# A hybrid decoder step on one core: seven pairs of its first projection with half the contraction in seven products of sums, variances inverted on 72 partitions, and two places in the gate reordered

## The chip, the cores and the metric

The kernel runs on one core of one Trainium2 chip. A core has engines with instruction streams of their own, each worked off strictly in order: TensorE (PE; its weight loads are counted as PEld), VectorE (DVE), ScalarE (ACT), GpSimd (POOL) and SyncE (SP), which here only issues DMAs. POOL issues DMAs too, on a queue of its own. The metric is the device time of one execution in microseconds (us), as the median of the runs.

## The reference, cut to what matters

576 tokens (512 of a prompt, and 8 sequences of 8 samples) go through one layer with 2048 channels. Channels are kept on the partitions, tokens on the free axis.

```python
h = rmsnorm(x, g_mix)
z = h @ w_in                                   # 2048 x 4096: a_val, a_gate, u, v
a = a_val * sigmoid(a_gate)                    # group A: 8 heads of 128 channels
a_out = silu(head_layernorm(causal_dwconv(concat(hist, a), w_dw_a, b_dw_a)))   # 31 taps
u = gelu(u); v_n = head_layernorm(gelu(v))     # group B: 8 heads of 128 channels
b_out = u * (tril(w_s[h]) @ v_n + b_s[h])      # over chunks of 128 positions
x = x + concat(a_out, b_out) @ w_out
up = rmsnorm(x, g_ffn) @ w_up                  # then a convolution of 3 taps, SiLU gate
x = x + (silu(conv(up)[:5632]) * conv(up)[5632:]) @ w_down
gate = sigmoid(rmsnorm(x, g_ple) @ w_ple_gate)
x = x + gate * (p @ w_ple_proj)
y = rmsnorm(x, g_final)                        # also the convolution states and v_n are outputs
```

`head_layernorm` subtracts the mean over a head's 128 channels and multiplies by 1/sqrt(variance + eps).

## The kernel before, in words

Every fp32 product is made from three matmuls: weights and activations are split into a high part and a rest (`wh`, `wl`, `xh`, `xl`), and `wh·xh + wh·xl + wl·xh` is summed in PSUM. One weight tile is 128x128, a token half is 288 columns, so a tile costs 6 matmuls of 288 columns, 3 for each half. The weights come in one stream of 512 KB units (8 tiles) on SP's queue into 5 buffers `raw`. A **piece** is 4 tiles: ACT makes `wh` of it (`prepare`, L279), then DVE makes `wl` (L283). There are 4 buffers of each, so the `wh` of piece s waits until PE has used piece s-4.

The stages in order, with the times of the trace: the first group (`gate(0)`, `val(0)`, `gate(1)` together, to 45 us); the rest of the first projection (to about 451 us), where for i = 2 to 7 the columns `vee(i-2)`, `you(i-2)` (v and u of group B), `gate(i)`, `val(i)` (group A) follow each other and `vee(6)`, `you(6)` come after them; a last group with `vee(7)` and `you(7)` together; `w_out` in two parts (`out` without the late channels `LATE`, then `out2`); the up-projection (680 to 1655 us), down-projection (to 2165 us), the gate in pairs of columns (to about 2316 us) and the two last gate columns with the final norm. The up-projection and the gate pairs already use the scheme that the change brings to the first projection: products of sums of weight tiles with sums of activations, seven for eight (`seven`, L879 to L881).

A main loop emits the matmuls in this order. After every 4 tiles it calls `deal()`, which hands out side work against a credit: first one step from `chain`, then steps from `urgent` or `todo`, each with a cost. `settle()` takes steps until a condition holds. A scheduler at compile time then fixes the order of each engine's instructions: it goes by the order of emission and by when its own model of times thinks an operand is ready. On the chip each engine holds to that order. `tc.issue_after(x)` keeps an instruction behind x.

The side work of group A's head i: `gated` (sigmoid), `val_done` (multiply, and `settle` until head i-3 has ended), then 31 `tap`s. Each tap is two DVE instructions, one on the prompt (L499, 128x512) and one on the samples (L501, 128x64). Then the steps of `chain`: `parts_of`, `centre` (PE and ACT), `square`, `spread` (PE sums the squares with a matrix of ones, ACT takes the root on all 128 partitions, L534), `norm(0)`, `norm(1)` (DVE: RECIPROCAL 128x288, L538, and a multiply, L539) and `fin` (ACT Silu, L543). Group B's head j: `vee_done` (multiply with the RMS factor `r`, L556, Gelu L558 and L559, then `norm`: PE `vps`, ACT L571, DVE `vn`), `you_done`, `mixing` (PE `mps`, DVE).

In the gate, `rms_roots` puts 576 roots on one partition, sends them through DRAM to 72 partitions of 8 (L1007, L1009), and `rms_spread` inverts them there (L1014) and sends them through DRAM to all 128 partitions (L1016, L1018) as `rg`; `gate_done` multiplies by it (L1033). In the tail, `split_12` makes activations of the last columns (ACT L1271, DVE L1272), and L1294 multiplies.

## Time and profile before

| | us |
|---|---|
| median of 3 runs (lowest, highest) | 2378.31 (2376.51, 2378.56) |
| the profiled execution | 2374.55 |
| its span on the core | 2372.9 |
| PE busy | 2353.6 (99%), 17676 matmuls |
| DVE busy | 2065.7 (87%), 3696 instructions |
| ACT busy | 1262.5 (53%), 2342 instructions |
| POOL busy | 265.4 (11%), 414 instructions |

The profile is one execution; its time is the span and what lies around it. A busy PE means that a matmul was under way. Matmuls overlap, so a matmul's own duration is longer than its share of the time. A row of instructions gives the start, the duration, the engine, the line and the tiles, and in brackets how long the engine was idle before it and what ended that.

### The profile page before, as it was taken

To read this page: it belongs to the slowest core of one execution; us is meant where nothing else is said; L and a number is where in the kernel's file an instruction comes from. 1 tells how busy PE (TensorE), PEld (TensorE's weight loads), DVE (VectorE), ACT (ScalarE), POOL (GpSimd) and SP (SyncE) were. 2 spreads that over 40 slices of the span, in tenths; PEclk is the share of its full clock that TensorE was granted. 3 is DMA by queue.
4 is the path that set the end of the run, shared out by engine and by line. 5 is a ranking of instruction groups with operands and counts; after the bars stand their busy time and mean duration, and the time that the engine had idled before them with its cause. 6 is when DMAs were issued, how large, how long until landed. Compare 5 with 4: busy or idle time off the path is not lost.

```text
span 2372.9 us, 45975 instructions
## 1 busy us (share of the span) xinstructions
PE 2353.6 (99%) x17676; PEld 2342.5 (99%) x17676; DVE 2065.7 (87%) x3696; ACT 1262.5 (53%) x2342; POOL 265.4 (11%) x414
## 2 busy tenths in 40 slices
PE   9999999999999999999999999999999999999997
PEld 9999999999999999999999999999999999999997
DVE  7877788887789999999999999999878998778997
ACT  6444544523575555555555555556545455456556
POOL 1000000000120000000000000000222332322112
PEclk9999999999999999999999999999999999999999
DMA  7322222333473333333333333335877776765546
GB/s 246 98 87 82 81 87 80 112 121 101 165 252 108 115 109 117 115 105 110 116 107 110 115 106 110 116 104 169 233 163 172 164 193 160 167 192 171 171 163 221
DMA packets 126392, 326.91 MB, mean 138 GB/s; under 512 B 29580, under 2 KB 46092, under 8 KB 126172
## 3 DMA queue, kind: packets, MB, share of 16 engines
q1 hardware_dynamic: 83068, 230.66, 29.5%
q0 software_dynamic: 37776, 82.68, 14.2%
q10 hardware_dynamic: 5328, 10.63, 1.4%
q8 instruction: 139, 2.28, 0.4%
q14 instruction: 81, 0.66, 0.1%
HBM read 260.45 MB, written 63.46 MB: 137 GB/s over the span
## 4 chain that ended last, share of the span: by engine, by line
PE 93%; issue 2%; DMA 2%; DVE 1%; ACT 1%; POOL 1%; DVEq 0%; POOLq 0%; ACTq 0%
PE acc_up L880 14%; PE acc_up L879 14%; PE acc_up L881 14%; PE acc L1209 10%; PE acc L1211 10%; PE acc L1213 10%; PE acc L839 5%; PE acc L840 5%; PE acc L838 5%; PE acc_gate L879 2%; PE acc_gate L881 2%; PE acc_gate L880 2%; DMA xs<-x1d 0%; POOL x1d L1248 0%; ACT wh L279 0%
## 5 line engine op out<-in xcount | busy, mean ns | idle before, releaser
L279 ACT ACTIVATE wh<-raw 128x512 fp32r<-128x512 f32 x792 | 499.2, 632 | 667.1 <-PE acc L1211 335.7
L879 PE MATMUL acc_up<-sx,wh 128*128 128x288 f32 x2464 | 726.9, 295 | 0.3 <-DVE uu L810 0.3
L881 PE MATMUL acc_up<-sx,wl 128*128 128x288 f32 x2464 | 727.0, 295 | 0.1
L880 PE MATMUL acc_up<-sx,wh 128*128 128x288 f32 x2464 | 726.8, 295 | 0.0
L283 DVE TENSOR_TENSOR wl<-raw,wh 128x512 fp32r<-128x512 f32 x792 | 541.1, 685 | 125.9 <-ACT wh L279 121.7
L879 PEld LDWEIGHTS acc_up<-sx,wh 128*128 128x128 f32 x2464 | 463.9, 188 | 0.6 <-issue 0.5
L880 PEld LDWEIGHTS acc_up<-sx,wh 128*128 128x128 f32 x2464 | 463.9, 188 | 0.1
L881 PEld LDWEIGHTS acc_up<-sx,wl 128*128 128x128 f32 x2464 | 463.1, 188 | 0.6 <-DVE wl L283 0.6
L1209 PE MATMUL acc<-xh,wh 128*128 128x288 f32 x1536 | 330.4, 296 | 0.7 <-ACT wh L279 0.6
L1211 PE MATMUL acc<-xl,wh 128*128 128x288 f32 x1536 | 327.5, 294 | 0.0
L1213 PE MATMUL acc<-xh,wl 128*128 128x288 f32 x1536 | 327.3, 294 | 0.0
L279 ACT ACTIVATE wh<-sy 128x512 fp32r<-128x512 f32 x268 | 170.1, 635 | 232.7 <-PE acc_up L880 155.6
L839 PE MATMUL acc<-sxh,wh 128*128 128x288 f32 x896 | 264.5, 295 | 0.0
L840 PE MATMUL acc<-sxh,wl 128*128 128x288 f32 x896 | 264.2, 295 | 0.0
L838 PE MATMUL acc<-sxh,wh 128*128 128x288 f32 x896 | 264.0, 295 | 0.0
L1209 PEld LDWEIGHTS acc<-xh,wh 128*128 128x128 f32 x1536 | 245.6, 188 | 2.8 <-issue 0.9
L1211 PEld LDWEIGHTS acc<-xl,wh 128*128 128x128 f32 x1536 | 246.5, 188 | 0.3 <-issue 0.2
L1213 PEld LDWEIGHTS acc<-xh,wl 128*128 128x128 f32 x1536 | 245.7, 188 | 0.4 <-issue 0.3
L283 DVE TENSOR_TENSOR wl<-sy,wh 128x512 fp32r<-128x512 f32 x268 | 183.8, 686 | 44.9 <-ACT wh L279 44.3
L499 DVE SCALAR_TENSOR_TENSOR cv<-ep,vec,cv 128x512 f32<-128x512 f32 x240 | 178.6, 744 | 0.0
L840 PEld LDWEIGHTS acc<-sxh,wl 128*128 128x128 f32 x896 | 168.6, 188 | 0.0
L838 PEld LDWEIGHTS acc<-sxh,wh 128*128 128x128 f32 x896 | 168.5, 188 | 0.0
(725 smaller groups left out, 3788.4 us busy)
## 6 DMA issues: line engine op xcount, KB each, us to landing
raw<-in_wstream SPq DMA_DIRECT2D x395, 512.0 KB
x1d<-o POOLq DMA_DIRECT2D x128, 144.0 KB, 4.7
hidd<-hp POOLq DMA_DIRECT2D x44, 288.0 KB, 3.8
xs<-x1d POOLq DMA_DIRECT2D x32, 288.0 KB, 3.9
hq<-hidd ACTq DMA_DIRECT2D x32, 288.0 KB
x<-in_xT SPq DMA_DIRECT2D x16, 288.0 KB
xr<-in_xT SPq DMA_DIRECT2D x16, 288.0 KB
x1d<-x POOLq DMA_DIRECT2D x16, 288.0 KB, 3.5
```

The costliest lines, as they stand in the source:

```text
L279: latest["h"] = nc.scalar.activation(h, src, AF.Copy).ins
L283: latest["l"] = nc.vector.tensor_tensor(out=l, in0=src, in1=h.bitcast(F32), op=ALU.subtract).ins
L499: tc.keep_in_program_order(nc.vector.scalar_tensor_tensor(out=cp, in0=halves(ep[:, k : k + SEQ]), scalar=w, in1=cp, op0=ALU.mult, op1=ALU. ...
L838: nc.tensor.matmul(dst, wh, bh, start=k == 0 and not on, stop=False, skip_group_check=on)
L839: nc.tensor.matmul(dst, wh, bl, start=False, stop=False, skip_group_check=on)
L840: nc.tensor.matmul(dst, wl, bh, start=False, stop=end, skip_group_check=on)
L879: nc.tensor.matmul(place[prod], wh, bh, start=k == 0 and not on, stop=False, skip_group_check=on)
L880: nc.tensor.matmul(place[prod], wh, bl, start=False, stop=False, skip_group_check=on)
L881: nc.tensor.matmul(place[prod], wl, bh, start=False, stop=k == KT // 2 - 1, skip_group_check=on)
L1209: nc.tensor.matmul(accs[n][:, h, :HT], wh, bh[:, h, :], start=st, stop=False)
L1211: nc.tensor.matmul(accs[n][:, h, :HT], wh, bl[:, h, :], start=False, stop=False)
L1213: nc.tensor.matmul(accs[n][:, h, :HT], wl, bh[:, h, :], start=False, stop=sp)
```

## The change

Four things are changed.

1. **Pairs.** For j = 0 to 6 `vee(j)` and `you(j)` form one group `both`. Over k = 0 to 7 (`SUMMED`) the 32 weight tiles (two columns, two token halves) go through seven products, each of a sum of weight tiles with a sum of activation halves (4 x 3 matmuls each: 84 in place of 96). The other 8 k are multiplied plainly (96), in pieces `A0`, `A1`, `B0`, `B1` of 24 matmuls that stand between the products (`MIXED`). A pair has 180 matmuls in place of 192, and 11 pieces in place of 8. DVE adds the weights in place in `raw` (`add_in_place`, 4 of 128x512 a pair), ACT and DVE keep partial results (`kept`) and combine them (`done_a`, `done_b`). The sums of activations (`mix_sums`) are made once, after the first group.
2. **Variances.** `spread` takes the root on one partition only; the 576 roots go through DRAM to 72 partitions of 8, are inverted there, go through DRAM to 128 partitions, and one DVE multiply of 128x576 uses them: four DMAs for each head on POOL's queue. The chains of heads 5 to 7 begin only in the last group.
3. **Room and other places for side work.** The samples' taps are multiplied on ACT (248 instructions of 128x64) and summed on DVE by 32 TENSOR_REDUCE of 9 or fewer taps; results of the heads that aren't late go to DRAM and come back for `w_out` (12 reloads); rows and mixing weights are loaded for each head on POOL's queue rather than at the start on SP's.
4. **Gate and tail.** `rms_spread` is called at the fifth product of the first pair (2 in `PRODS`), not the fourth (7), `rg` is used behind the latest `wl`, and a pause follows. In the tail `split_12` comes after the first half column, behind the latest pieces.

The instructions that move, as each engine executes them (line, operation, output<-inputs with the tile's number, shape):

DVE where head 4 of group A is normalised, before (`wl` are pieces of weights, `cv` and `lnc` the head's root and centred values, `ep` and `es` the next head's convolution):

```order
L477 TENSOR_TENSOR es_4546<-acc_0_4381,ag_4377 128x8x8
L283 TENSOR_TENSOR wl_4555<-raw_4277,wh_4554 128x512
L499 SCALAR_TENSOR_TENSOR cv_4412<-ep_3311,vec,cv_4412 128x2x256
L538 RECIPROCAL cv_3756<-cv_3756 128x288 x2
L539 TENSOR_TENSOR lnc_4481<-lnc_4481,cv_3756 128x288 x2
L501 SCALAR_TENSOR_TENSOR cv_4412<-es_3312,vec,cv_4412 128x2x32
L499 SCALAR_TENSOR_TENSOR cv_4412<-ep_3311,vec,cv_4412 128x2x256
L501 SCALAR_TENSOR_TENSOR cv_4412<-es_3312,vec,cv_4412 128x2x32
```

The same head on DVE now (`vr` holds the 576 values on 72 partitions, `gu` and `kept` belong to the pairs, `raw` are the weights that are added in place):

```order
L322 TENSOR_TENSOR wl_4818<-raw_4553,wh_4817 128x512
L609 RECIPROCAL vr_4493<-vr_4493 72x8
L779 TENSOR_TENSOR gu_4808<-gu_4808,r 128x576
L269 TENSOR_TENSOR raw_4553<-raw_4553,raw_4555 128x512 x2
L769 TENSOR_TENSOR kept_0_4815<-acc_4814,kept_0_4815 128x288
L322 TENSOR_TENSOR wl_4854<-raw_4553,wh_4853 128x512
L322 TENSOR_TENSOR wl_4875<-raw_4611,wh_4874 128x512
L322 TENSOR_TENSOR wl_4891<-raw_4555,wh_4890 128x512
L617 TENSOR_TENSOR lnc_4469<-lnc_4469,cv_3873 128x576
L665 RECIPROCAL vs_4787<-vs_4787 128x4
L561 TENSOR_SCALAR cv_5807<-ep_3845,vec 128x2x256
```

Two reciprocals of 128x288 and two multiplies stood back to back; now one of 72x8 and one multiply of 128x576, with three pieces and the pair's sums between them, and directly behind the multiply stands what group B's `vn` needs.

ACT behind that multiply now (`junk`, `vs` are group B's variances; L621 is the head's Silu; `kept_1` a pair's partial result):

```order
L664 ACTIVATE vs_4787<-vs_4787,eps_t 128x4
L664 ACTIVATE vs_4787<-vs_4787,eps_t 64x1
L621 ACT_TABLE_LOAD
L621 ACTIVATE lnc_4469<-lnc_4469,vec 128x576
L809 ACTIVATE kept_1_4816<-acc_4813 128x288
L318 ACTIVATE wh_4908<-raw_4611 128x512
L318 ACTIVATE wh_4928<-raw_4643 128x512
```

The Silu needs the multiply, and the copy of the pair's product 5 (`five` in the code) and the next `wh` stand behind it; before, the same Silu had only `wh` pieces behind it:

```order
L543 ACT_TABLE_LOAD
L543 ACTIVATE mix_4543<-lnc_4481,vec 128x576
L279 ACTIVATE wh_4656<-raw_4415 128x512
L279 ACTIVATE wh_4694<-raw_4415 128x512
L279 ACTIVATE wh_4752<-raw_4494 128x512
```

DVE in the first gate pair, before (L1033 uses the factors `rg`; `sx`, `sy` and the adds of L228 prepare the next pair's weights):

```order
L228 TENSOR_TENSOR sx_0_27221<-raw_27141,raw_27143 128x512
L1033 TENSOR_TENSOR g0b<-g0b,rg 128x576
L228 TENSOR_TENSOR sy_0_27223<-sx_0_27221,raw_27018 128x512
L228 TENSOR_TENSOR raw_27141<-raw_27141,raw_27018 128x512
L810 TENSOR_TENSOR g0a<-acc_gate_26936,uug_26940 128x288
L1033 TENSOR_TENSOR g0a<-g0a,rg 128x576
```

and now (the same adds are L243, the pieces L322, the use of `rg` L1234):

```order
L243 TENSOR_TENSOR sy_0_27573<-sy_0_27573,raw_27495 128x512
L243 TENSOR_TENSOR sy_1_27598<-sx_1_27596,raw_27368 128x512
L243 TENSOR_TENSOR raw_27491<-raw_27491,raw_27368 128x512
L322 TENSOR_TENSOR wl_27601<-sy_1_27598,wh_27600 128x512
L322 TENSOR_TENSOR wl_27618<-sx_0_27571,wh_27617 128x512
L243 TENSOR_TENSOR sy_1_27598<-sy_1_27598,raw_27495 128x512
L322 TENSOR_TENSOR wl_27636<-sx_1_27596,wh_27635 128x512
L322 TENSOR_TENSOR wl_27654<-raw_27491,wh_27653 128x512
L1234 TENSOR_TENSOR g0a<-g0a,rg 128x576
```

The use of `rg` stood between the first of the next pair's sums; it now stands behind all of them and behind five pieces.

The diff, cut to its core:

```diff
+RATE_BOTH = 0.15, 1.4
...
+SUMMED = range(8)
+MIXED = [1, 6, 2, 5, 7, "A0", 4, "A1", "B0", 3, "B1"]
...
-        add("mix", "w_in", [vee(i - 2)], ks)
-        add("mix", "w_in", [you(i - 2)], ks)
         add("mix", "w_in", [gate(i)], ks)
         add("mix", "w_in", [val(i)], ks)
-    add("mix", "w_in", [vee(NB - 2)], ks)
-    add("mix", "w_in", [you(NB - 2)], ks)
+        add("both", "w_in", [vee(i - 2), you(i - 2)], ks)
+    add("both", "w_in", [vee(NB - 2), you(NB - 2)], ks)
...
+        elif phase == "both":
+            (w, a), (_, b) = outs
+            for m, odd in ((a, 0), (b, 0), (b, 1), (a, 1)):
+                tiles += [(w, k, m) for k in SUMMED[odd::2]]
+            for m in (a, b):
+                tiles += [(w, k, m) for k in ks if k not in SUMMED]
+            pieces += [(n // UNIT + 2 + "AB".index(x[0]), int(x[1])) if isinstance(x, str)
+                       else (n // UNIT, x, None) for x in MIXED]
...
+        q = [slot(u, n) for n in range(4)]
+
+        def put(n, a, b, op=ALU.add):
+            nc.vector.tensor_tensor(out=q[n], in0=q[a], in1=q[b], op=op)
+
+        if prod == 6:
+            put(1, 1, 2)
+            put(0, 1, 0)
+        if prod == 7:
+            put(1, 0, 2, ALU.subtract)
+        if prod == 3:
+            put(0, 0, 3)
+        summed_w[s] = q[{1: 0, 6: 0, 2: 3, 5: 1, 7: 1, 4: 2, 3: 0}[prod]]
+
     summed_w, added, latest = {}, set(), {}
...
+        def sample(k):
...
+            w, x = v("w_dw_a", i * TAPS + k), es[:, :, k : k + DS]
+            if k == 0:
+                nc.scalar.activation(out, x, AF.Identity, bias=v("b_dw_a", i), scale=w)
+            else:
+                nc.scalar.activation(out, x, AF.Copy, scale=w)
+            if k == TAPS - 1:
+                add_samples(box["new"], n + 1, box["c"][:, :, 256:HT])
+
...
+        def add_samples(t, n, out):
+            nc.vector.tensor_reduce(out=out, in_=t[:, :n, :].rearrange("p k (a b) -> p a b k", a=2),
+                                    op=ALU.add, axis=mybir.AxisListType.X)
...
         def spread():
-            box["s"] = box["c"]
+            row = box["c"][:1]
             for h in range(2):
-                nc.scalar.activation(box["s"][:, h, :], summed(ones_r, h, "var"), AF.Sqrt, bias=eps_t)
-
-        def norm(h):
-            x, f = box["cc"][:, h, :], box["s"][:, h, :]
-            nc.vector.reciprocal(f, f)
-            nc.vector.tensor_tensor(out=x, in0=x, in1=f, op=ALU.mult)
+                nc.scalar.activation(row[:, h, :], summed(ones_r, h, "var")[:1, :], AF.Sqrt, bias=eps_t[:1])
+            d = dram.tile([TOK // 8, 8], F32, tag=f"root{i}", name=f"root{i}")
+            nc.gpsimd.dma_start(d.rearrange("a (o b) -> o (a b)", o=1), row.rearrange("p a b -> p (a b)"))
+            box["s"] = tl([TOK // 8, 8], "hist", f"vr{i}", bufs=2)
+            nc.gpsimd.dma_start(box["s"], d)
+
+        def invert():
+            with tc.issue_after(latest["l"]):
+                nc.vector.reciprocal(box["s"], box["s"])
+            d = dram.tile([TOK // 8, 8], F32, tag=f"factor{i}", name=f"factor{i}")
+            nc.gpsimd.dma_start(d, box["s"])
+            nc.gpsimd.dma_start(box["c"].rearrange("p a b -> p (a b)"),
+                                d.rearrange("a (o b) -> o (a b)", o=1).to_broadcast([P, TOK]))
+
+        def norm():
+            with tc.issue_after(latest["l"]):
+                nc.vector.tensor_tensor(out=box["cc"], in0=box["cc"], in1=box["c"], op=ALU.mult)
 
         def fin():
-            m = tl([P, 2, HT], f"hd{LATE.index(i)}" if i in LATE else f"res{i}", f"mix{i}")
+            m = tl([P, 2, HT], f"hd{LATE.index(i)}", f"mix{i}") if i in LATE else box["cc"]
             nc.scalar.activation(m, box["cc"], AF.Silu, bias=v("b_ln_a", i), scale=v("g_ln_a", i))
+            if i not in LATE:
+                nc.gpsimd.dma_start(mix_d[i], m)
             mix[i] = m
 
         for k in range(TAPS):
             todo.append((0.74, lambda k=k: tap(k)))
         def begin():
+            if i >= LATE[0] and not state.get("plain"):
+                waiting.append(begin)
+                return
+            rest = (0.0, lambda: None)
             chain.extend([(0.7, lambda: parts_of(box["c"])), (0.0, centre), (0.7, square), (0.0, spread),
-                          (2.2, lambda: norm(0)), (2.2, lambda: norm(1)), (0.0, fin)])
+                          rest, rest, (0.1, invert), rest, rest, rest, (0.7, norm), (0.0, fin)])
...
+        def add_in():
+            e, o = (tmp(f"xm{2 * q + n}") for n in range(2))
+            for n, g in enumerate((e, o)):
+                nc.scalar.activation(g, x0[2 * q + n], AF.Copy, scale=v("g_mix", 2 * q + n))
+            ta, tb = tmp(f"tam{q}"), tmp(f"tbm{q}")
+            nc.vector.tensor_tensor(out=ta[:, 0, :], in0=e[:, 0, :], in1=e[:, 1, :], op=ALU.subtract)
+            nc.vector.tensor_tensor(out=ta[:, 1, :], in0=o[:, 1, :], in1=ta[:, 0, :], op=ALU.add)
+            nc.vector.tensor_tensor(out=tb[:, 0, :], in0=e[:, 1, :], in1=o[:, 1, :], op=ALU.subtract)
+            nc.vector.tensor_tensor(out=tb[:, 1, :], in0=o[:, 0, :], in1=ta[:, 1, :], op=ALU.subtract)
+            box.update(a=ta, b=tb)
...
+        for what in MIXED:
+            if isinstance(what, str):
+                t, half = (X, Y)["AB".index(what[0])], int(what[1])
+                for k in plain[half * SUB : (half + 1) * SUB]:
+                    wh, wl = weights()
+                    for w, part in ((wh, 0), (wh, 1), (wl, 0)):
+                        for h in range(2):
+                            fresh = t is Y and h == 1 and k == plain[0] and w is wh and part == 0
+                            nc.tensor.matmul(t[:, h, :HT], w, of_half(k, h)[part], start=fresh,
+                                             stop=k == plain[-1] and w is wl, skip_group_check=True)
+                state["rate"] = RATE_BOTH[1]
+            else:
+                t, h = place[what]
+                on = what not in (1, 5, 6)
+                for q in range(len(SUMMED) // 2):
+                    wh, wl = weights()
+                    xa, xb = quarter_of(what, q)
+                    end = q == len(SUMMED) // 2 - 1
+                    nc.tensor.matmul(t[:, h, :HT], wh, xa, start=q == 0 and not on, stop=False, skip_group_check=on)
+                    nc.tensor.matmul(t[:, h, :HT], wh, xb, start=False, stop=False, skip_group_check=on)
+                    nc.tensor.matmul(t[:, h, :HT], wl, xa, start=False, stop=end, skip_group_check=on)
+                state["rate"] = RATE_BOTH[0]
+            deal(what in ("A0", "A1", "B0", "B1", 2, 7, 3))
+            if what == 1:
+                nc.scalar.activation(first, X[:, 0, :HT], AF.Copy)
+            if what == 6:
+                sub(u, Y[:, 0, :HT], first)
+            if what == 5:
+                nc.scalar.activation(five, X[:, 1, :HT], AF.Copy)
+            if what == 7:
+                sub(z, Y[:, 0, :HT], first)
+                sub(z, z, five)
+            if what == 3:
+                vee_done(a - 3 * NA, done_a)
+        you_done(b - 2 * NA, done_b)
...
-            nc.vector.tensor_tensor(out=t, in0=t, in1=r["t"], op=ALU.mult)
+            with ExitStack() as order_of:
+                if m < 2:
+                    order_of.enter_context(tc.issue_after(latest["l"]))
+                nc.vector.tensor_tensor(out=t, in0=t, in1=r["t"], op=ALU.mult)
...
-            if m == 0 and prod == 7:
+            if m == 0 and prod == 2:
                 settle(lambda: "t" in roots)
                 rms_spread()
...
+        if m == 0:
+            todo.append((1.5, lambda: None))
...
-        nc.scalar.activation(t[:, 0, :], src, AF.Copy, scale=scale)
-        nc.vector.scalar_tensor_tensor(out=t[:, 1, :], in0=src, scalar=scale, in1=t[:, 0, :].bitcast(F32),
-                                       op0=ALU.mult, op1=ALU.subtract)
+        with tc.issue_after(latest["h"]):
+            nc.scalar.activation(t[:, 0, :], src, AF.Copy, scale=scale)
+        with tc.issue_after(latest["l"]):
+            nc.vector.scalar_tensor_tensor(out=t[:, 1, :], in0=src, scalar=scale, in1=t[:, 0, :].bitcast(F32),
+                                           op0=ALU.mult, op1=ALU.subtract)
...
-    todo.extend((0.5, lambda k=k: split_12(k)) for k in evens)
...
     with tc.issue_after(sig[LAST[0], 0]):
         scale_half(0, rest)
+    todo.extend((0.5, lambda k=k: split_12(k)) for k in evens)
     gate_half(LAST[1], 0)
```

More of the change, by code (lines that the diff above doesn't have):

```diff
@@ L252, in trunk_kernel @@
     late_sums = {s for s, p in enumerate(pieces) if len(p) == 3 and p[1] == 6 and p[0] in late_units}
+    own_time = {s for s, p in enumerate(pieces) if len(p) == 3 and p[2] is None and p[1] in (6, 7)}
     def prepare(s):
@@ L257, in prepare @@
         for a in range(s, s + 3):
-            if a == s or a not in late_sums:
+            if a == s or a not in late_sums and a not in own_time:
                 add_up(a)
@@ L431, in take, with deal @@
         state["credit"] -= cost
-    def deal():
+    def deal(step=True):
         state["credit"] += state["rate"]
-        if chain:
+        if chain and step:
             take(chain)
@@ L452, in seqs @@
         return ap.rearrange("p a (b c) -> p a b c", c=DS)
-    res, mix = {}, {}
+    res, mix, mixes = {}, {}, {}
+    mix_d = [dram.tile([P, 2, HT], F32, tag=f"mixd{k}", name=f"mixd{k}") for k in range(KT)]
     held = {}
@@ L594, in you_done @@
         g = tmp(f"gu{j}")
-        nc.vector.tensor_tensor(out=g, in0=acc[:, :, :HT], in1=r["t"], op=ALU.mult)
+        times_r(g, acc)
         nc.scalar.activation(g, g, AF.Gelu_apprx_tanh)
@@ new lines, in mix_sums, with parts_in @@
+    def mix_sums(q):
+        box = {}
+        def add_in():
[8 more added lines that the diff above has]
+            box.update(a=ta, b=tb)
+        def parts_in(name, n):
+            h, l = (tl([P, 2, HT], MSUMS[4 * q + n + a], f"sm{q}_{n + a}", dt=F32R) for a in range(2))
+            nc.scalar.activation(h, box[name], AF.Copy)
+            nc.vector.tensor_tensor(out=l, in0=box[name], in1=h.bitcast(F32), op=ALU.subtract)
+            one, two = (5, 6) if name == "a" else (7, 4)
+            sums_m[one, q] = h[:, 0, :], l[:, 0, :]
+            sums_m[two, q] = h[:, 1, :], l[:, 1, :]
+        return [(1.8, add_in), (0.7, lambda: parts_in("a", 0)), (0.7, lambda: parts_in("b", 2))]
@@ L1162, in trunk_kernel @@
             state["rate"] = RATE3 if final else RATE1
+            if final:
+                state["plain"] = True
+                while waiting:
+                    todo.appendleft((0.0, waiting.pop()))
+                for k in EARLY:
+                    if k in mix:
+                        load_mix(k)
         if phase == "out":
@@ L1230, in trunk_kernel @@
             r["t"] = rms()
+            for q in range(len(SUMMED) // 2):
+                urgent.extend(mix_sums(q))
         for n, (w, m) in enumerate(outs):
```

149 lines of the change are left out of this document (102 added, 47 removed).

## The prediction

> **What bounds the kernel now.** I read the page's first part, then what PE waits for, then busy time by stage, then the groups by form of the first projection, and last the timelines of the places that the change touches. The page:
>
> ```profile
> span 2372.9 us, 45975 instructions
> PE 2353.6 (99%) x17676; PEld 2342.5 (99%) x17676; DVE 2065.7 (87%) x3696; ACT 1262.5 (53%) x2342; POOL 265.4 (11%) x414
> PE 93%; issue 2%; DMA 2%; DVE 1%; ACT 1%; POOL 1%; DVEq 0%; POOLq 0%; ACTq 0%
> ```
>
> PE is busy 99% of the span and carries 93% of the chain that ended last. So a matmul that goes is worth its share of PE's time, and other work counts only where PE waits for it. The stretches (PE, PEld, DVE, ACT, POOL busy, then the clock, DMA share and GB/s) and all that PE waits for:
>
> ```profile
> 45.00:600.00 555.00, 554.97 (x4177) 550.47 (x4178) 449.00 (x887) 240.10 (x420) 26.41 (x42) 1.00 0.29 95
> 2165.00:2200.00 35.00, 32.52 (x234) 30.92 (x233) 30.49 (x54) 20.30 (x34) 7.60 (x14) 1.00 0.53 171
> ...
> PE acc L1294 <- DVE wl L283: 1.8, 2, 0.9
> PE acc_gate L881 <- DVE wl L283: 1.5, 2, 1.4
> PE acc_gate L879 <- ACT wh L279: 0.9, 1, 0.9
> ```
>
> In the first projection and `w_out` PE idles 0.03 us of 555; nothing can be gained there but by fewer matmuls, and every new wait is a loss. The gate's first pair holds 2.4 us of waits, the tail (L1294) 1.8. DVE has 449 of 555 us filled, ACT 240.
>
> **Part by part: the matmuls.** The pitch of a matmul is read from starts in the first projection, not from durations, since matmuls overlap:
>
> ```profile
> 90.04 0.42 PE L1209 MATMUL acc<-xh,wh 128*128 128x288 f32 x2
> 90.31 0.42 PE L1211 MATMUL acc<-xl,wh 128*128 128x288 f32 x2
> 90.57 0.43 PE L1213 MATMUL acc<-xh,wl 128*128 128x288 f32 x2
> 90.84 0.42 PE L1209 MATMUL acc<-xh,wh 128*128 128x288 f32 x2
> ```
>
> Six matmuls take 90.84 - 90.04 = 0.80 us, 0.133 us each. Seven pairs lose 12 each: 84 x 0.133 = 11.2 us, at full clock. This is the certain term, since PE has no slack there that could swallow it.
>
> **The engines that feed PE.** The rows by form of 45 to 600 us, DVE and ACT, and from the page a load from DRAM on POOL's queue:
>
> ```profile
> L283 DVE TENSOR_TENSOR wl<-raw,wh 128x512 fp32r<-128x512 f32 x165 | 112.8, 685 | 60.7 <-ACT wh L279 59.6 <-DMA raw<-in_wstream 0.9
> L501 DVE SCALAR_TENSOR_TENSOR cv<-es,vec,cv 128x64 f32<-128x64 f32 x240 | 66.5, 277 | 0.0
> L538 DVE RECIPROCAL cv<-cv 128x288 f32<-128x288 f32 x16 | 30.4, 1929 | 5.9 <-ACT cv L534 5.9
> L539 DVE TENSOR_TENSOR lnc<-lnc,cv 128x288 f32<-128x288 f32 x16 | 6.7, 429 | 0.0
> ...
> L279 ACT ACTIVATE wh<-raw 128x512 fp32r<-128x512 f32 x164 | 103.8, 633 | 279.2 <-PE acc L1211 273.3 <-ACT ag L461 1.7 <-DVE r L349 1.5
> L559 ACT ACTIVATE gw<-gv 128x64 f32<-128x64 f32 x8 | 1.9, 240 | 0.0
> ...
> xs<-x1d POOLq DMA_DIRECT2D x32, 288.0 KB, 3.9
> ```
>
> DVE loses 66.5 + 30.4 + 6.7 = 104 us. It gains 21 more `wl` (21 x 0.685 = 14), 28 adds of the same shape (19), 8 multiplies of 128x576 (8 x 0.75 = 6), some 72 small sums and multiplies of 128x288 for the pairs and the sums of activations (x 0.43 = 31) in place of seven of 128x576 (5), eight of 128x576 for the sums of activations (6), and 32 reductions, which the trace of before does not hold. One reads up to 576 elements a partition: between 0.277 us (the tap's row) and 1.93 us (the slowest row of that size or less); I take 0.75 as for a multiply of 128x576, 24 us, with 9 and 62 as the ends. Sum: 95 us against 104; at the ends 80 and 133, and DVE would still stand at 478 of 544. ACT gains 248 x 0.24 = 60 us of taps, 21 x 0.633 = 13 of `wh` and some 15 of copies: 330 of 544. Neither becomes a bound on average; both are costed at nothing, covered by `wh` buffers that today wait for PE (273 of 279 us of idle before L279). If that cover fails at one place in every pair, a piece late by 0.3 us costs 2 us in all, and I put 1 us into the sum for it, for the sums of activations right after the first group included. The 12 reloads and the rows move to POOL's queue, which is at 26 of 555 us; reloads of their size land in 3.9 us (last row), and the order has them over 10 us ahead of use: nothing. The Trainium skill (VectorE: DVE Perf Modes, Rules for kernel authors) calls a reduction the slowest DVE operation, to be kept off the hot path; no row here shows one, and only the high end of 62 us allows for it.
>
> **The variances: the new waits.** The trace has this path once, in the gate: root on one partition, DRAM, 72 partitions, reciprocal, DRAM, 128 partitions.
>
> ```profile
> 2174.17 0.88 ACT L1005 ACTIVATE roots<-rps,eps_t 1x288 f32<-1x288 f32 x2
> ...
> 2175.34 0.54 POOL L1007 DMA_DIRECT2D roots<-roots  x1 [0.49 <-ACT roots L1005]
> 2178.27 0.55 POOL L1009 DMA_DIRECT2D roots<-roots  x1 [1.83 <-DMA roots<-roots]
> 2182.93 0.53 POOL L1016 DMA_DIRECT2D factors<-roots  x1 [4.11 <-DVE roots L1014]
> 2186.31 0.55 POOL L1018 DMA_DIRECT2D rg<-factors  x1 [2.85 <-DMA factors<-roots]
> ...
> 2182.43 0.20 DVE L1014 RECIPROCAL roots<-roots 72x8 f32<-72x8 f32 x1 [1.26 <-DMA roots<-roots]
> 2189.82 0.76 DVE L1033 TENSOR_TENSOR g0b<-g0b,rg 128x576 f32<-128x576 f32 x1 [1.70 <-DMA rg<-factors]
> ```
>
> From the end of the root (2175.05) to the reciprocal 7.4 us, from its end to the multiply 7.2: a double hop is 7.3 us where DMA is busy 0.53. In the first projection it is busy 0.29, and small stores land sooner (the DMA issues of 45 to 470 us, median us to landing last; below them a load that stands among the gate's hops):
>
> ```profile
> out_chunk_v_prompt<-vn POOLq DMA_DIRECT2D x8, 64.0 KB, 2.0
> out_chunk_v_sample<-vn POOLq DMA_DIRECT2D x8, 32.0 KB, 2.7
> ...
> xr<-x1d POOLq DMA_DIRECT2D x4, 288.0 KB, 3.7
> ```
>
> Two landings at 2.0 and the 1.0 us that the gate's hops have around theirs make 5.0, the low end; 2.45 for each, the middle of these two rows, makes 5.9, which I take, as nearer to this stage; 7.3 is the high end. The Trainium skill (DMA: Bandwidth & Descriptors, Anatomy of one DMA — SWDGE (gpsimd) path) gives about 2.0 us fixed for a DMA, mostly the wait for the write's receipt; two would be about 4 us, no head would then wait, and the sum would be that of rival A. The gate's rows are 1.8 times that.
>
> Heads 0 to 4 run through this inside pairs, and the reciprocal and the multiply stand at fixed places on DVE. Behind a waiting one stand `wl` pieces and group B's `vn`, for which PE's `mps` waits, and on ACT, behind the Silu, the copy of product 5 and the next `wh`. For head 4 the order has three pieces between root and reciprocal and three between reciprocal and multiply. A product's piece is 12 matmuls, 1.59 us, so there is room for 6 x 1.59 = 9.5 us, 9.3 with what the reserve of pieces adds and the Silu behind it takes. The same count over the orders of heads 0 to 3 gives 10.6, 11.6, 10.9 and 10.8 us (my estimate, some 0.7 us each way). Two hops of 5.9 are 11.8: 1.2 + 0.2 + 0.9 + 1.0 + 2.5 = 5.8 us of waits. At 5.0 (10.0) it is 0.7, at 7.3 (14.6) it is 4.0 + 3.0 + 3.7 + 3.8 + 5.3 = 19.8. Heads 5 to 7 have the same chain in the last group with steps of rest, and `w_out` needs their results only in its second part: nothing.
>
> **Gate and tail.** In the gate DVE waits 1.70 us for `rg` (row above), with the next pair's sums and pieces queued behind, and then PE waits:
>
> ```profile
> 2194.27 0.40 PE L881 MATMUL acc_gate<-sg,wl 128*128 128x288 f32 x1 [1.38 <-DVE wl L283]
> 2196.80 0.40 PE L879 MATMUL acc_gate<-sg,wh 128*128 128x288 f32 x1 [0.94 <-ACT wh L279]
> ```
>
> Now the reciprocal comes one product later (24 matmuls, 3.2 us) and five pieces stand ahead of the multiply; what is late next is only the sigmoid, which nobody needs soon. I take 2.2 of 2.3 us; between 0 and 2.5. In the tail an ACT instruction waits for a load, with all `wh` behind it:
>
> ```profile
> 2327.93 0.54 ACT L1271 ACTIVATE x<-xs,vec 128x288 fp32r<-128x288 f32 x1 [4.18 <-DMA xs<-x1d]
> ```
>
> It moves behind the last pieces, which ends the two waits of 0.9 us; its 8 results are then made while PE does a half column (48 x 0.133 = 6.4 us), 8 x 0.54 = 4.3 us on ACT: just in time. 1.5 us, between -1 and 1.8.
>
> **The sum** on the profiled execution: 2374.55 - 11.2 - 2.2 - 1.5 + 5.8 + 1.0 = 2366.5. The median of the runs lies 3.8 us above the profiled execution (2378.31), and the forecast, for a median, is 2378.3 - 8.1, rounded to 2370.
>
> **The rivals.** *A, no waits:* the hops take 5.0 us or less, or PE's reserve is larger than I counted: 2378.3 - 14.9 + 0.7 = 2364. For it: DMA share 0.29, 2.0 us landings. Against it: no DMA of this four-hop kind has been seen so fast, and 3 us landings stand beside. *B, the gain is eaten:* hops of 6.6 us give 5 x 13.2 - 53.2 = 12.8 us of waits: 2378.3 - 14.9 + 12.8 + 1 = 2377. For it: the gate's rows; a load of the weights' stream (512 KB) runs in between. Against it: the lower share. *C, slower:* the reciprocal's and the multiply's fixed places on DVE hold up the pieces; from a hop of 6.7 us the waits (5 x 13.4 - 53.2 = 13.8, and 1) eat the whole gain, from 7.2 the kernel is 0.2% slower, and 7.3 gives 2378.3 - 14.9 + 19.8 + 1 = 2384. For it: 7.3 is the only measured value. Against it: loads of 288 KB (last row above) were issued on the same queue among the gate's hops. *D, gate and tail don't do what they say:* the waits move on, 2370 + 3.7 = 2374.
>
> **How the numbers follow.** Forecast 0.38 (2366 to 2373 as its own range), A 0.24, B 0.16, C 0.14, D 0.08. Less than 0.2% (4.8 us) can't be told from no change: faster is below 2373.5. The forecast, A and some of D give 0.65 faster; B, the rest of D and a part of C within 0.2%, 0.22; the rest of C slower, 0.13. The range goes from 2362 (A with all gate and tail terms at their ends) to 2381 (half of C left out).
>
> **What would show it.** PE: 17592 or so recorded matmuls and no longer pitch in the pairs. DVE's `norm` rows (128x576, five before 451 us): idle before them, by DMA, of 1 to 2 us each, and PE rows with idle behind them; more than 3 us speaks for C, none for A. Root to reciprocal and reciprocal to multiply: 5.9 us each. Waits of L881 and L879 in the gate and of L1294 gone. It would be wrong if the pairs' `wl` come late by DVE's own work, or if PE waits in 45 to 72 us for the sums of activations.

## The result, and the profile after

The changed kernel takes 2390.84 us (median of 4 runs, 2390.04 to 2392.20) against 2377.41 us for the kernel before (4 runs): a ratio of 1.0063, 95% interval 1.0048 to 1.0077. It is 13.4 us slower; the forecast was 2370, the range 2362 to 2381. The page of the changed kernel's profiled execution:

```profile
span 2388.3 us, 46227 instructions
PE 2355.9 (99%) x17592; PEld 2340.4 (98%) x17592; DVE 2081.9 (87%) x3586; ACT 1336.9 (56%) x2635; POOL 315.1 (13%) x508
PE 87%; DVE 6%; issue 3%; DMA 2%; ACT 2%; POOL 0%; DVEq 0%; POOLq 0%; SPq 0%; ACTq 0%
```

PE has 84 matmuls fewer and is busy 2.3 us longer; its share of the chain that ended last fell from 93% to 87%, and DVE's rose to 6%. The stretches of the prediction again (PE, PEld, DVE, ACT, POOL busy, clock, DMA share, GB/s):

```profile
45.00:600.00 555.00, 539.24 (x3965) 528.91 (x3965) 460.95 (x770) 306.03 (x696) 70.32 (x124) 0.99 0.37 109
2165.00:2200.00 35.00, 35.00 (x261) 34.31 (x260) 32.90 (x59) 25.22 (x42) 9.19 (x18) 1.00 0.63 202
```

Where PE idled 0.03 us, it now idles 15.8 (555 - 539.24), and the clock is no longer 1.00 throughout. DVE has 461 us filled there against 449: more, not less. What PE waits for:

```profile
PE vps L656 <- ACT gw L648: 5.0, 2, 3.6
PE mps L694 <- DVE vn L673: 4.6, 4, 2.7
PE acc L789 <- ACT kept L809: 1.9, 1, 1.9
PE var L584 <- ACT lnh L577: 1.5, 2, 1.2
PE acc L799 <- DVE kept L769: 1.1, 3, 0.5
...
PE acc_up L1077 <- DVE uu L1008: 0.9, 1, 0.9
PE acc L801 <- DVE wl L322: 0.9, 2, 0.7
```

The waits of the gate and of the tail are gone; the four largest lie in the first projection, and they are for group B's results (`gw`, `vn`) and for the pairs' partial results more than for pieces of weights. The longest shows how it comes about. The DMAs of head 0, and DVE around them:

```profile
147.60 0.54 POOL L603 DMA_DIRECT2D root<-cv  x1 [5.21 <-ACT cv L601]
150.35 0.56 POOL L605 DMA_DIRECT2D vr<-root  x1 [2.22 <-DMA root<-cv]
154.73 0.53 POOL L611 DMA_DIRECT2D factor<-vr  x1 [3.81 <-DVE vr L609]
158.21 0.60 POOL L612 DMA_DIRECT2D cv<-factor  x1 [2.95 <-DMA factor<-vr]
```

```profile
154.23 0.20 DVE L609 RECIPROCAL vr<-vr 72x8 f32<-72x8 f32 x1 [1.24 <-DMA vr<-root]
...
162.45 0.76 DVE L617 TENSOR_TENSOR lnc<-lnc,cv 128x576 f32<-128x576 f32 x1 [5.52 <-DMA cv<-factor]
163.13 0.68 DVE L322 TENSOR_TENSOR wl<-raw,wh 128x512 fp32r<-128x512 f32 x1
...
169.65 0.45 DVE L774 TENSOR_TENSOR gv<-gv,r 128x288 f32<-128x288 f32 x1
```

The second double hop takes 8.0 us (154.43 to 162.45) and DVE stands still for 5.52 of them. From then to 169.65 it works without a gap at what has piled up, and `gv` comes at the end of that. PE, then its clock (the first row of the windows is idle; the clock is the third number from the end):

```profile
167.25 0.29 PE L1428 MATMUL acc<-xh,wl 128*128 128x288 f32 x1
171.18 2.08 PE L656 MATMUL vps<-cen,gw 128*128 128x128 f32 x8 [3.63 <-ACT gw L648]
...
174.69 0.69 PE L1426 MATMUL acc<-xl,wh 128*128 128x288 f32 x2
175.17 0.69 PE L1428 MATMUL acc<-xh,wl 128*128 128x288 f32 x2
```

```profile
169.00:170.00 1.00, 0.00 (x0) 0.00 (x0) 1.00 (x3) 0.98 (x2) 0.00 (x0) 1.00 0.84 279
...
172.00:173.00 1.00, 1.00 (x6) 0.96 (x5) 0.97 (x3) 0.28 (x2) 0.00 (x0) 0.50 0.03 8
...
177.00:178.00 1.00, 1.00 (x9) 1.00 (x8) 0.48 (x1) 1.00 (x5) 0.00 (x0) 0.93 0.03 12
```

Towards the end of 3.63 us of idle the clock falls to half and stays there until 177 us: two matmuls take 0.48 us (174.69 to 175.17), 0.24 each, against 0.133. From 45 to 600 us, 13.7 us pass at half clock, which costs 6.8, or 6.4 without the 0.9 us in which PE still waited. So a wait was paid for about 1.4 times. (In the experiments the loss to the half clock is half of the time at half clock; it counts a wait inside such a stretch twice, by up to 1.5 us, in experiment 3.)

The ledger by stages, from the starts of PE's rows:

| | before | change | difference |
|---|---|---|---|
| first group: its 288th matmul starts | 43.3 | 46.3 | +3.0 |
| from there to the first matmul of the up-projection (673.57, 692.66) | 630.3 | 646.4 | +16.1 |
| up-projection and down-projection | 1492.1 | 1494.8 | +2.7 |
| gate pairs | 162.2 | 158.7 | -3.5 |
| tail, to the matmuls of the final norm | 32.4 | 29.6 | -2.8 |

The second row is -11.2 of matmuls, +15.6 of idle, +6.4 of half clock, and 5.3 that no row shows as idle. Of these, 2.7 are the first matmul behind each of the 20 waits: the next one starts 0.29 us later rather than 0.133 (before: 3 waits, 0.5 us). The third row varied by as much between kernels with the same code there.

### The profile page after: what moved, and what is told of

Read it like the earlier page. It is cut to its first block, busy times and chain, and to the rows that moved or that the text cites. A ratio compares the mean times of both kernels' runs of the same rounds, so it can differ in the third digit from the quotient of the medians.

```text
span 2388.3 us, 46227 instructions
## 1 busy us (share of the span) xinstructions
PE 2355.9 (99%) x17592; PEld 2340.4 (98%) x17592; DVE 2081.9 (87%) x3586; ACT 1336.9 (56%) x2635; POOL 315.1 (13%) x508
## 4 chain that ended last, share of the span: by engine, by line
PE 87%; DVE 6%; issue 3%; DMA 2%; ACT 2%; POOL 0%; DVEq 0%; POOLq 0%; SPq 0%; ACTq 0%
PE acc_up L1078 13%; PE acc_up L1079 13%; PE acc_up L1077 13%; PE acc L1424 7%; PE acc L1428 7%; PE acc L1426 7%; PE acc L1037 5%; PE acc L1036 5%; PE acc L1038 5%; DVE cv L566 2%; PE acc_gate L1077 2%; PE acc_gate L1079 2%; PE acc_gate L1078 2%; PE acc L789 2%; DVE wl L322 1%
## 5 line engine op out<-in xcount | busy, mean ns | idle before, releaser
L318 ACT ACTIVATE wh<-raw 128x512 fp32r<-128x512 f32 x813 | 510.5, 632 | 585.6 <-PE acc L1426 199.3
L322 DVE TENSOR_TENSOR wl<-raw,wh 128x512 fp32r<-128x512 f32 x813 | 554.0, 684 | 114.7 <-ACT wh L318 109.4
L1424 PE MATMUL acc<-xh,wh 128*128 128x288 f32 x1088 | 235.5, 297 | 0.9 <-ACT wh L318 0.7
L1428 PE MATMUL acc<-xh,wl 128*128 128x288 f32 x1088 | 234.4, 296 | 0.0
L1426 PE MATMUL acc<-xl,wh 128*128 128x288 f32 x1088 | 233.6, 296 | 0.2 <-DVE xl L363 0.2
L322 DVE TENSOR_TENSOR wl<-sy,wh 128x512 fp32r<-128x512 f32 x268 | 183.3, 684 | 45.7 <-ACT wh L318 45.0
L1424 PEld LDWEIGHTS acc<-xh,wh 128*128 128x128 f32 x1088 | 176.0, 190 | 2.4 <-ACT wh L318 1.0
L1426 PEld LDWEIGHTS acc<-xl,wh 128*128 128x128 f32 x1088 | 175.8, 189 | 0.9 <-DVE xl L363 0.5
L1428 PEld LDWEIGHTS acc<-xh,wl 128*128 128x128 f32 x1088 | 175.6, 189 | 0.9 <-issue 0.7
```

The costliest lines, as they stand in the source:

```text
L318: latest["h"] = nc.scalar.activation(h, src, AF.Copy).ins
L322: latest["l"] = nc.vector.tensor_tensor(out=l, in0=src, in1=h.bitcast(F32), op=ALU.subtract).ins
L1424: nc.tensor.matmul(accs[n][:, h, :HT], wh, b[h][0], start=st, stop=False)
L1426: nc.tensor.matmul(accs[n][:, h, :HT], wh, b[h][1], start=False, stop=False)
L1428: nc.tensor.matmul(accs[n][:, h, :HT], wl, b[h][0], start=False, stop=sp)
```

## The experiments

Ratios are to runs of the kernel before on the same chip, whose medians were 2375.6 to 2376.4 us. The change itself was timed beside runs of before at 2377.41, so a difference to the change below, as a time, holds to some 1.5 us.

**1. The variances inverted as before.** The root again on all partitions, two reciprocals and two multiplies of 128x288 a head:

```diff
-            row = box["c"][:1]
+            box["s"] = box["c"]
             for h in range(2):
-                nc.scalar.activation(row[:, h, :], summed(ones_r, h, "var")[:1, :], AF.Sqrt, bias=eps_t[:1])
...
-                          rest, rest, (0.1, invert), rest, rest, rest, (0.7, norm), (0.0, fin)])
+                          (2.2, lambda: norm(0)), (2.2, lambda: norm(1)), (0.0, fin)])
```

> The changed kernel with the variances inverted as before (root on 128 partitions, two reciprocals of 128x288 and two multiplies on DVE for each head, no DMA); pairs, samples on ACT, reloads, gate and tail stay as changed. Theory H (the waits come from the DMA hops at the heads' fixed places on DVE): PE's waits in the first projection fall from 15.8 us to under 4 and the half-speed stretches (6.8 us) go; about 2370 us, against 2391 for the change and 2377 for before. Rival P (the pairs themselves, their partial results and sums are late): at least 10 us of waits stay, 2385 or more. Rival S (samples on ACT, reductions on DVE): as P, 2385 or more.

2378.30 us (10 runs), ratio 1.0014 (1.0005 to 1.0024): 12.5 us less than the change. Half of theory H's expectation: the waits for `gw` and `vn` fall to 0.5 and 0.3 us, but PE still idles 9.3 us and loses 3.4 to the half clock.

```profile
PE var L584 <- ACT lnh L577: 2.6, 4, 1.1
PE acc L787 <- DVE gv L757: 2.3, 1, 2.3
PE acc L789 <- DVE wl L322: 1.6, 3, 0.8
PE acc L777 <- DVE wl L322: 1.3, 1, 1.3
```

These are late DVE results and pieces with no DMA in front of them. DVE from 45 to 460 us, here and before:

```profile
45.00:460.00 415.00, 405.67 (x2983) 396.16 (x2982) 383.26 (x642) 263.23 (x628) 54.52 (x96) 0.99 0.33 103
```

```profile
45.00:460.00 415.00, 414.97 (x3115) 410.46 (x3116) 340.94 (x692) 193.27 (x348) 26.41 (x42) 1.00 0.28 90
```

383 of 415 us are filled (92%), against 341 (82%).

**2. Only the taps forced.** In the changed kernel the end of a `val` column forces out the whole chain of head i-3, so its steps of rest do nothing for heads 0 to 4; here it forces only the taps:

```diff
-        settle(lambda: i < 3 or i - 3 in mix)
+        settle(lambda: i < 3 or i - 3 in tapped)
...
         def begin():
+            tapped.add(i)
```

> The changed kernel, but the multiplication of a val column no longer forces the whole chain of head i-3 out; it only forces its taps, so the chain's steps of rest act for heads 0 to 4 too, and the multiply by the factors stands behind group B's vn on DVE. The same four DMAs a head. Theory H: DVE's wait ahead of the multiply (12.4 us in all) goes nearly to 0, PE's waits fall to under 5 us, about 2370 us. Rival P or S: PE's waits stay at 10 us or more, 2385.

2380.44 us, ratio 1.0021 (1.0011 to 1.0030), 10.4 less than the change. The hop ahead of the multiply is hidden (45 to 460 us, the change and then here):

```profile
L617 DVE TENSOR_TENSOR lnc<-lnc,cv 128x576 f32<-128x576 f32 x5 | 3.8, 758 | 12.4 <-DMA cv<-factor 12.4
L618 DVE TENSOR_TENSOR lnc<-lnc,cv 128x576 f32<-128x576 f32 x5 | 3.8, 754 | 0.6 <-DMA cv<-factor 0.6
```

12.4 us of DVE's waiting became 0.6; ahead of the reciprocal it still waits 4.1 us, against 7.7. PE still idles 11.8 us, not under 5, and loses 3.4 to the clock. One place, ACT and then DVE:

```profile
312.17 2.19 ACT L318 ACTIVATE wh<-raw 128x512 fp32r<-128x512 f32 x4 [4.66 <-DVE raw L269]
```

```profile
309.66 0.75 DVE L567 SCALAR_TENSOR_TENSOR cv<-ep,vec,cv 128x512 f32<-128x512 f32 x1
310.32 0.55 DVE L562 TENSOR_SCALAR cv<-ep,vec 128x512 f32<-128x512 f32 x1
310.78 0.75 DVE L567 SCALAR_TENSOR_TENSOR cv<-ep,vec,cv 128x512 f32<-128x512 f32 x1
311.44 0.69 DVE L269 TENSOR_TENSOR raw<-raw,raw 128x512 f32<-128x512 f32 x1
```

ACT waits 4.66 us for a sum of weights that stands behind taps of the convolution on a DVE without a gap. This gave theory B: DVE is too late where forced taps meet the pair's own sums.

**3. The pairs multiplied plainly**, variances through DRAM. The pairs keep the place that the change gives them, behind `gate(i)` and `val(i)` rather than ahead:

```diff
-        add("both", "w_in", [vee(i - 2), you(i - 2)], ks)
+        add("mix", "w_in", [vee(i - 2)], ks)
+        add("mix", "w_in", [you(i - 2)], ks)
...
-            for q in range(len(SUMMED) // 2):
-                urgent.extend(mix_sums(q))
```

> The changed kernel with the seven pairs multiplied plainly (192 matmuls each, no sums), in the order gate, val, vee, you; variances through DRAM, samples on ACT, reloads, gate and tail as changed. Theory H: the DMA waits stay on DVE (5 to 15 us), since the chains are forced at the same place; PE has 11.2 us more of matmuls and larger pieces to cover with: 2380 to 2395. Rival P: without the pairs no waits are left, and with the gate's and tail's gain it is about 2371.

2396.61 us, ratio 1.0091 (1.0076 to 1.0106), 1.6 us beyond theory H's range and in its direction: without the pairs the waits stay.

```profile
PE vps L658 <- ACT gw L650: 11.6, 2, 5.9
PE vps L658 <- ACT gw L651: 2.7, 1, 2.7
```

DVE stood 11.4 us for `cv<-factor` and 4.0 for `vr<-root`; PE idled 17.9 us and lost 8.5 to the half clock. DVE is filled only 314 of 415 us here, so the hops need no full DVE to make PE wait. The new place of the pairs is in this kernel too and was not tried alone.

**4. Only the gate's and the tail's edits**, on the kernel before. Besides these lines, the steps behind the first gate pair begin with an empty one, and the tail's `split_12` steps are queued behind the first half of the first of the last two gate columns rather than ahead of it:

```diff
-            nc.vector.tensor_tensor(out=t, in0=t, in1=r["t"], op=ALU.mult)
+            with ExitStack() as order_of:
+                if m < 2:
+                    order_of.enter_context(tc.issue_after(latest["l"]))
+                nc.vector.tensor_tensor(out=t, in0=t, in1=r["t"], op=ALU.mult)
...
-            if m == 0 and prod == 7:
+            if m == 0 and prod == 2:
...
-        nc.scalar.activation(t[:, 0, :], src, AF.Copy, scale=scale)
+        with tc.issue_after(latest["h"]):
+            nc.scalar.activation(t[:, 0, :], src, AF.Copy, scale=scale)
```

> The kernel before with only the edits of the gate and the tail. All theories: the waits of 2.4 us in the gate's first pair and of 1.8 us in the tail go; minus 3.5 to 4.2 us, about 2373.5. If the trace of the change misleads and they moved on, no difference.

2368.93 us, ratio 0.9972 (0.9963 to 0.9982): faster than both kernels, by 6.8 us, more than expected. None of the waits of L881, L879 and L1294 is left. By the starts of PE's rows the gate pairs take 158.7 us rather than 162.2 and the tail 29.6 rather than 32.4: 6.3 us, of which PE's waits had shown 4.2.

**5. More taps earlier** (and the first rows on SP's queue as in experiment 13, and one and two steps of rest ahead of the reciprocal and the multiply rather than two and three), on experiment 2:

```diff
-RATE1, RATE2, RATE3 = 1.65, 1.7, 1.0
+RATE1, RATE2, RATE3 = 2.2, 1.7, 1.0
-RATE_BOTH = 0.15, 1.4
+RATE_BOTH = 0.3, 1.6
```

> As the run in which only taps are forced, with three more edits: the rows of the first two heads of group B are loaded on SP's queue behind the start's own loads; taps are handed out faster (rate 2.2 for 1.65 in gate and val, 0.3 and 1.6 for 0.15 and 1.4 in the pairs), so that fewer are forced at the end of a val column, where DVE then has the pair's in-place sums behind them; one and two steps of rest in place of two and three. Theory B (what is left are bursts of forced taps ahead of the pair's sums and pieces): PE's waits and half-speed stretches fall from 15.2 us to under 7; first group 2.5 us shorter; about 2369. Rival P (the pairs' own chain of partial results): waits stay at 13 or more, 2378 by the start alone.

2373.47 us, ratio 0.9993 (0.9983 to 1.0002): 7 us less than experiment 2, but with one rest DVE waits 9.9 us for the first hop, and PE's waits and half clock are 11.5, not under 7. B in part.

**6 and 7. The samples' taps back on DVE**, on experiment 2 and on experiment 1 (no reductions; the first rows on SP's queue in both):

```diff
-            sample(k)
+            cs = box["c"][:, :, 256:HT]
+            tc.keep_in_program_order(nc.vector.scalar_tensor_tensor(
+                out=seqs(cs), in0=es[:, :, k : k + DS].rearrange("p (a b) c -> p a b c", a=2),
+                scalar=w, in1=seqs(cs), op0=ALU.mult, op1=ALU.add))
```

> As the run in which only taps are forced, with the samples' taps back on DVE (240 of 128x64, no reductions) and the first rows on SP's queue. Theory S (samples on ACT and the reductions of 1.2 us on DVE make pieces late): waits fall from 15.2 us to under 7, about 2370. Theory B: DVE has 48 us of small taps for 35 us of reductions, the waits stay or grow, 2378 or more. The start gains 2.5 us in all theories.

> Variances and samples as before, the first rows on SP's queue; what stays of the change are the pairs, the reloads, the gate and the tail. Theory S: 2366 to 2370. Theory B or P: DVE gets the reciprocals and the samples' taps back and has more to do than in any other run here: waits of 13 us or more, 2376 or more.

2404.84 us (ratio 1.0126, 1.0111 to 1.0141) and 2396.66 (1.0092, 1.0077 to 1.0107): theory S falls, the samples on ACT are a relief. In the first of the two PE waits at four places for the same thing:

```profile
PE cen L595 <- ACT lnh L588: 31.2, 4, 8.3
```

`lnh` needs the last tap, and the forced taps are now twice as many instructions.

**8 and 9. 20 of the 31 taps left out**, which takes work from DVE and ACT (116 and 27 us from 45 to 600 us in experiment 8): on experiment 1 (no hops) and on the changed kernel (hops). The rest is handed out at the same steps, but the order that is fixed at compile time is not quite the same: 592 of DVE's 668 other instructions ahead of the up-projection keep it in experiment 8, 587 of 652 in experiment 9. One execution each.

```diff
-            if k == TAPS - 1:
+            if k == 10:
...
-            todo.append((0.74, lambda k=k: tap(k)))
+            todo.append((0.74, (lambda k=k: tap(k)) if k < 11 else (lambda: None)))
```

> The run with the variances inverted as before, with 20 of the 31 taps of the convolution left out (prompt on DVE, samples on ACT; steps of the same cost that do nothing stand in their place, so the rest is handed out as before). Leaves DVE and ACT some 110 and 55 us less to do. Theory B (DVE is too late with what stands in order ahead of the pair's sums and pieces): waits and half-speed stretches fall from 12.8 us to under 3. Rival P (partial results on the way between PE, ACT and DVE): they stay at 9 or more.

> The changed kernel with the same 20 taps left out; the DMA hops stay. Theory H: DVE gets to the reciprocal and the multiply earlier and waits longer there (over 25 us in all), PE's waits and half-speed stretches stay at 8 us or more. Theory B alone, without H: they fall under 3 us as in the run beside it.

With these two the four corners are there, as the start of the up-projection on PE:

| first matmul of the up-projection, us | all taps | 11 taps |
|---|---|---|
| DMA hops (the change, experiment 9) | 692.66 | 680.70 |
| no hops (experiments 1 and 8) | 682.09 | 670.22 |

The hops cost 10.6 us with all taps and 10.5 with 11, beyond what the reciprocals on DVE cost that they replace; the 20 taps, on DVE and ACT and in the order, cost 12.0 and 11.9. The two add up, and neither needs the other. Each corner is one profile, and the match to 0.1 us is luck: counted from the end of the first group it is 10.1 and 10.8, 11.6 and 12.3, and over the whole of these four executions the hops cost 11.7 and 8.9, with later stages that differ by up to 3 us between kernels with the same code there. In experiment 8 PE's waits are down to

```profile
PE acc L777 <- DVE wl L322: 2.2, 5, 0.5
```

and little else (2.8 us idle, full clock); from the first group to the up-projection it takes 624.0 us, 6.3 less than before. That is what the pairs bring when DVE is free: 11.2 less 2.8 of waits and 2.1 that no row shows as idle. Rival P falls with it. In experiment 9 DVE waits longer ahead of the multiply:

```profile
L617 DVE TENSOR_TENSOR lnc<-lnc,cv 128x576 f32<-128x576 f32 x5 | 3.8, 759 | 19.8 <-DMA cv<-factor 19.8
```

Ahead of the reciprocal it waits 0.9 us, so 20.6 in all against 20.1 in the change, not over 25 as expected; PE's waits and half clock, 13.5 us, stay as theory H has it.

**10 and 11. Both causes mended.** Experiment 1 with only taps forced and rates 2.4, 0.3 and 1.6; and experiment 5 with three rests ahead of the reciprocal and three ahead of the multiply. Both have the first rows on SP's queue, which experiment 13 tries alone, so not all of their gain is the two causes. Both with:

```diff
-                assert i < 2 or i - 2 in mix
+                settle(lambda: i < 2 or i - 2 in mix)
...
-                          rest, (0.1, invert), rest, rest, (0.7, norm), (0.0, fin)])
+                          rest, rest, rest, (0.1, invert), rest, rest, rest, (0.7, norm), (0.0, fin)])
```

(the second piece in experiment 11 alone).

> Variances as before, only taps forced at a val column's end, taps handed out faster (2.4; 0.3 and 1.6 in the pairs), first rows on SP's queue. No hops and smaller bursts: theory B and H together: waits under 6 us, about 2368, as fast as the kernel before with gate and tail alone; if the reciprocals' 27 us of DVE decide: 2376 or more.

> The variances through DRAM, with three steps of rest ahead of the reciprocal and three ahead of the multiply, only taps forced, rates 2.2, 0.3 and 1.6, first rows on SP's queue. Against the run with one and two rests: DVE's wait for the first hop (9.9 us) goes under 3; PE's waits and half-speed stretches from 11.4 to under 7; about 2369.

2370.39 us (ratio 0.9977, 0.9968 to 0.9987) and 2371.49 (0.9983, 0.9974 to 0.9993): some 20 us less than the change, faster than before, and no faster than the gate's and the tail's edits alone. In experiment 11 DVE waits for no hop at all; what is left in both (8.0 and 9.4 us of idle and half clock, expected under 6 and under 7) is spread over six kinds of late results in each, with DVE filled 382 and 371 of 415 us. Experiment 10 fills DVE as experiment 1 does (383) and loses 4 to 5 us less in waits and half clock: the order of the taps counts beside the fill.

**12. The pairs' sums of weights on POOL**, on experiment 10.

```diff
-            nc.vector.tensor_tensor(out=q[n], in0=q[a], in1=q[b], op=op)
+            nc.gpsimd.tensor_tensor(out=q[n], in0=q[a], in1=q[b], op=op)
```

> As the run with the variances as before and faster taps, with the pairs' 28 in-place sums of weights on POOL rather than DVE: DVE has 19 us less to do in the first projection. If DVE's load is what makes the pairs' pieces late, the waits (8.0 us) fall under 4 and the time to about 2366, below the kernel before with the gate's and tail's edits alone; if POOL takes more than some 2 us for a sum or its sums stand behind DMAs in its order, they grow instead, 2373 or more.

2388.49 us, ratio 1.0051 (1.0036 to 1.0066). The sums are slower there:

```profile
L269 POOL TENSOR_TENSOR raw<-raw,raw 128x512 f32<-128x512 f32 x21 | 34.1, 1625 | 102.5 <-DMA raw<-in_wstream 36.2 <-DVE wl L322 25.3 <-DVE gv L763 19.9
```

1.6 us for 0.69 on DVE, and in the order of a queue that waits for other things. It tells nothing on how much DVE's load costs.

**13. The first rows on SP's queue**, the only edit to the change.

```diff
-        nc.gpsimd.dma_start(t[:, 0, :], A["wsT"][:, j, :])
+        with ExitStack() as order_of:
+            if j < 2:
+                order_of.enter_context(tc.issue_after(loaded))
+            queue = nc.sync if j < 2 else nc.gpsimd
+            queue.dma_start(t[:, 0, :], A["wsT"][:, j, :])
...
```

> The changed kernel with one edit: the rows of the first two heads of group B are loaded on SP's queue behind the start's loads, not on POOL's queue at 2 us. If those 8 loads cost the first group its 2.7 us, the first 288 matmuls start by 43.2 us rather than 45.6, and the time is 2388; if the half-speed stretch at the start has another cause, 2390.5 as the change.

2383.02 us, ratio 1.0032 (1.0020 to 1.0043): 7.8 less than the change. In the changed kernel POOL's engine is free at 2 us and issues eight loads for the first two heads of group B from 2.06 to 8.06 us, in the middle of the first activations' loads (DMA issues of the change from 0 to 12 us, then SP's row that waits until a load of activations has landed and holds back the next loads):

```profile
rows<-in_wsT POOLq DMA_DIRECT2D x2, 64.0 KB, 5.7
rows<-in_b_s POOLq DMA_DIRECT2D x2, 64.0 KB, 6.2
```

```profile
8.71 0.24 SPq L410 DMA_DIRECT2D seen<-x  x1
```

In experiment 13 that row stands at 6.06 us, 2.65 earlier:

```profile
6.06 0.24 SPq L410 DMA_DIRECT2D seen<-x  x1
```

In the one profile the first group is 1.3 us shorter and the stretch behind it 2.6, where DVE waits 11.6 us for the hops rather than 20.1. Its first matmuls still run at half speed until about 9 us, and how long they do so differs between kernels with the same code there (the 48th matmul starts at 11.7 to 13.8 us in the seven kernels besides before and experiment 4 with these rows on SP's queue); that part of the 3.0 us, and why the time fell by more than the profile shows, stays open.

## Why the prediction was wrong

The direction was wrong, and not through the rival that was to end there. Point by point:

- **The matmuls, 11.2 us.** The count and the pitch were right: a product's matmuls start 0.1325 us apart. But "PE has no slack there that could swallow it" was only half of it: with DVE free, experiment 8 keeps 6.3 of 11.2.
- **"Neither becomes a bound on average; both are costed at nothing."** This step failed, by the 12.0 us that experiments 1 and 8 lie apart, against the 1 us in the sum for a failing cover: the largest error. The sign was named ("if the pairs' `wl` come late by DVE's own work") and given no price and no chance. First in size: DVE in 45 to 600 us was to fall by 9 us and rose by 12. A good half of this is the reductions: 1.19 us each where 0.75 was taken:

```profile
L549 DVE TENSOR_REDUCE smp<-smp 128x64 f32<-128x576 f32 x24 | 28.4, 1185 | 0.9 <-ACT smp L544 0.6
L549 DVE TENSOR_REDUCE cv<-smp 128x64 f32<-128x448 f32 x8 | 7.7, 960 | 0.0
```

  36.1 us for 24, inside the bounds that were given but only used for an average. The 12.0 us are what leaving out 20 taps gains, not the price of what the change adds; how much of them is the reductions, the pairs' sums or the order in which forced taps meet them was not separated. Then in kind: an average over 544 us holds the last stretch, where DVE has time. In 45 to 460 us DVE's work and its waits for the hops fill 380 of 415 us (359.5 and 20.1), and in a pair the forced taps and the pair's sums meet. The cover that I named, `wh` waiting for PE, was there on average (273 us before) and not at these places: ACT waits 21.0 us for sums that DVE makes (`raw`, L269).
- **The hops, 5.8 us.** The mechanism was right and the size wrong: they cost 10.6 us. The five first hops took 6.9, 8.4, 8.7, 5.5 and 5.6 us from the end of the root to the reciprocal (the fourth: to its landing), the five second ones 8.0, 6.0, 6.0, 6.7 and 5.7: 6.75 on average, not 5.9, with a spread that the estimate by one number left out. By its own formula 6.75 gives 14.3 us; the runs show 10.6. These twenty DMAs landed 1.6 to 4.8 us after their issue, 3.0 on average. The Trainium skill (DMA: Bandwidth & Descriptors, Anatomy of one DMA — SWDGE (gpsimd) path) gives about 2.0 us fixed for a DMA; with that alone no head would have waited, and this trace does not bear it out.
- **The clock was not in the sum.** 6.4 us of the 22.2 that PE lost to waits and clock are matmuls at half clock after waits; they are part of both prices above. No row of before shows this in the first projection, where PE waits only 0.03 us.
- **"The 12 reloads and the rows move to POOL's queue … nothing."** Wrong for the rows of the first two heads. I looked at how full the queue is (and the 26 us are POOL's busy time), not at when an engine with nothing else to do would issue them.
- **Heads 5 to 7: nothing.** Right; their multiplies wait for no DMA.
- **Gate and tail, 2.2 and 1.5 us.** Right in kind and too small: 6.8 us together by experiment 4. The tail's end of -1 was needless.
- **The rivals.** C named the hops' price alone, at 7.3 us a hop; it came out slower through two causes of about equal size. Each alone stays inside the range (2378.30 us in experiment 1, 2376.74 in experiment 9), both together do not. B and C held 0.30, too little, since nothing in them allowed for DVE's own load.

## What to carry to other kernels

When PE is filled to 99%, price a change that gives PE less and its helpers more by the helpers' fill in the stretch where the work lands, with their waits counted as filled, and by what stands in order ahead of PE's next operand, not by the average of a stage. The fill is a sign and no price: experiments 1 and 10 fill DVE alike and lose 12 and 8 us. A round trip through DRAM belongs behind the work that PE needs next, with room for its slowest instance: moved there (experiment 2), the same four DMAs cost DVE 0.6 us rather than 12.4 ahead of the multiply, at the same DVE fill (362 and 360 of 415 us). And a change of several parts is to be split: here two small edits were worth 6.8 us alone, and the rest cost 20.
